# Hybrid encoder with a mixture of experts: gathers for two rounds at a time, 19 weight slots for 17, light and heavy rounds alternating

## The chip, the cores and the metric

The kernel runs on one core of one Trainium2 chip. The metric is the device time of one execution in microseconds. Loads of weights are issued by SyncE (SP) into one queue, and 16 DMA engines move them; TensorE (PE) multiplies, VectorE (DVE), ScalarE (ACT) and GpSimd (POOL) do the rest.

## The reference

Two layers are computed on 256 tokens of width 1024, in float32. Each layer first mixes tokens (a projection, banded attention, a state-space scan, retention, an output projection); then come 32 experts, of which each token uses the best two of its best group:

```python
for i in range(DEPTH):
    ...
    x = x + g1 * mixed
    h = _rmsnorm(x, norm2_g[i]) * (1.0 + sc2) + sh2
    x = x + g2 * _hier_moe(h, ...)
return _rmsnorm(x, final_g)

def _hier_moe(h, w_group, ..., w_down):
    group_idx = jnp.argmax(group_logits, axis=-1)
    ...
    top_val, top_idx = lax.top_k(in_group, TOP_K)       # 2 of the group's 8 experts
    ...
    for gi in range(N_GROUPS):
        hg = jnp.einsum('nd,edf->nef', t, w_gate[e])    # 1024 -> 256
        hu = jnp.einsum('nd,edf->nef', t, w_up[e])
        act = jax.nn.silu(hg) * hu * combine[:, e, None].astype(t.dtype)
        out = out + jnp.einsum('nef,efd->nd', act, w_down[e])   # 256 -> 1024
```

## The kernel before

Each layer has a mix phase and an expert phase. The expert phase of a layer reads all 32 experts: per expert two tiles of 1 MB with the gate and up weights (`wgu`, issued on L134) and one of 1 MB with the down weights (`moe_w_down`, L142), 96 loads in all. SP issues them in order in one queue. Each takes the next slot of a ring by turn (`wslot`, L120 to L128): 8 slots `ring2`, 7 slots `w`, 2 slots `ring3`, so 17. A slot is free again when the matmuls that read its last tile are done, and a load whose slot is not free holds up SP and every load behind it. In layer 0 eight loads for the next layer take the eight `ring2` slots first.

The expert phase begins with the routing (`route`): logits, the two experts of each token, and for each expert the place of each of its tokens. Experts are then worked off in 11 rounds, which fill 128 columns each: three fixed rounds with experts 0 to 5, two each with 64 token slots; then the other 26 experts, sorted by how many tokens they have (`order`, L1061 to L1100, 26x26 comparisons on DVE): three heavy rounds of two experts with 64 slots and five light rounds of four experts with 32 slots. So fixed and heavy rounds need 6 loads each and light ones 12. The order is fixed x 3, heavy x 3, light x 5. The sorted expert numbers (`numi`) are read into SP's registers by a TENSOR_LOAD (L1124); loads of experts 6 to 31 stand behind it in SP's queue and take their address from it.

Rounds take their tokens from blocks. A gather (L1142 to L1170) makes one: DVE writes a 0/1 matrix (`matrix`, L1109, in a `b4` buffer of 512 columns), PE multiplies the tokens with it (L1159; 32 matmuls, 8 row pieces of 128 x 4 terms), DVE and ACT write the result, scaled and shifted, into eight `b2` buffers of 128x512. Block 0 holds the three fixed rounds (256 columns ahead of round 0, 128 more behind its first product), block 1 rounds 3 to 6, block 2 rounds 7 to 10.

A round is then, on PE in the order written by `run` (L1266 to L1306): `slots` (two transposes, L1180, which give each slot's weight and the matrix for the way back), `gate_up` (L1195, 32 or 64 matmuls over 512 columns), `turned` (two transposes, L1207), `down` (L1220, 16 or 32 matmuls) and `scatter` (L1249 and L1250, 8 matmuls that add the result to the tokens). A fixed or heavy round's `down` comes behind the next round's `gate_up`, a light one's in its own round. Ahead of a gather the outstanding `down` is done, behind the gate and up product of the round the outstanding scatters.

After block 1 (round 6) stands the overflow branch (`between`, L1349 and on): a `tc.If` on the largest count (`cmi`), with the general code for experts with more than 64 tokens. On these inputs it isn't taken, but all engines evaluate it.

PE follows the program's order in the rounds; SP's loads are placed by the scheduler by when they become due, with loads of experts known ahead free to move forward, and those that need `numi` behind its TENSOR_LOAD.

Of the kernel before, what the change touches and what calls it, by code (L numbers as in the profile page):

```python
# [21 lines left out]
D = 1024  # L22
NE = 32
# [3 lines left out]
FIX, HEAVY, LIGHT = 6, 6, 32  # L27
DYN = NE - FIX
EPS = 1e-6
PRIO = 200  # L30
NW = 7
NW2 = 8
NW3 = 2

# [16 lines left out]
def body(tc, I, O):  # L51
# [3 lines left out]
    with tc.tile_pool(name="cp", bufs=1) as cp, tc.tile_pool(name="ring", bufs=NW) as ring, \  # L55
# [3 lines left out]
        def nm(s):  # L59
# [887 lines left out]
        def route(l, filler, scaled):  # L947
# [5 lines left out]
            def turned(h, t):  # L953
                xT[h, t] = b2([128, 512])
# [54 lines left out]
            m1, at1, f1 = first_max(ev, "a")  # L1009
            oh1, oh2 = sb([128, 10, 8], "oh1"), sb([128, 10, 8], "oh2")  # L1010
            V.tensor_tensor(oh1, at1, wide(f1), op=ALU.is_equal)
# [24 lines left out]

            def weights():
                V.tensor_tensor(oh2, at2, wide(f2), op=ALU.is_equal)
                m5 = m1.rearrange("p (t g) -> p t g", t=2)
# [13 lines left out]
                V.tensor_tensor(w2, w1, e, op=ALU.mult)  # L1053
                wa, both = sb([128, 10, 8], "wa"), sb([128, 10, 8], "both")
                for o, oh, w in ((wa, oh1, w1), (both, oh2, w2)):
# [5 lines left out]
            def order():  # L1061
# [8 lines left out]
                V.scalar_tensor_tensor(key, cnt[:, FIX:NE], 64.0, own, op0=ALU.mult, op1=ALU.subtract)  # L1070
                sq = [128, DYN, DYN]
                tmp, oh = sb(sq, "sqa"), sb(sq, "sqb")
# [4 lines left out]
                V.tensor_tensor(oh, C("iota")[:, 0:DYN].unsqueeze(2).to_broadcast(sq),  # L1077
                                rank[:, None, :].to_broadcast(sq), op=ALU.is_equal)

                def sorted_(dst, src):  # L1080
                    V.tensor_tensor(tmp, oh, src[:, None, :].to_broadcast(sq), op=ALU.mult)
                    V.tensor_reduce(dst, tmp, axis=AX.X, op=ALU.add)

# [29 lines left out]
        def experts(posm, comb, xhi, xlo, a2, sh2, gr2, l, ahead=True, D0=None, between=None, order=None, more=True,  # L1113
# [8 lines left out]
            if ahead:  # L1122
                numi, posd, comd = order
                _, num = nc.values_load_multi_w_load_instructions(  # L1124
                    numi[0:1, :], engines=(mybir.EngineType.SP,), min_val=FIX, max_val=NE - 1,
                    skip_runtime_bounds_check_because="sums of a permutation's 0/1 rows times FIX..NE-1")
                i = 0
                while i < NE:
                    n, w = (2, CAP) if i < FIX + HEAVY else (4, LIGHT)
                    r = len(rounds)  # L1130
# [4 lines left out]
                    i += n  # L1135
            else:
                for r in range(16):
                    j = slice(2 * r, 2 * r + 2)
                    rounds.append((r // 4, r % 4 * 128, CAP, posm[:, :, j], comb[:, :, j], [2 * r, 2 * r + 1]))
            last = {r[0]: i for i, r in enumerate(rounds)}  # L1140

            def gather(blk):  # L1142
                Dm[blk] = b4([128, 2, 512], F32R)
                for b, po, w, pos, _, _ in rounds:
                    if b == blk:
                        matrix(Dm[blk], po, pos, w)
                gathered(blk, slice(0, rounds[last[blk]][1] + 128), 1)

            def gathered(blk, ss, n):
                pc = {}  # L1150
                w = ss.stop - ss.start
                for c0 in range(0, 8, n):
# [17 lines left out]
            def slots(r):  # L1170
# [11 lines left out]
                V.tensor_reduce(cw, tp[:, 0:256], axis=AX.X, op=ALU.add)  # L1182
                sT = b1_([128, 256], F32R)
                V.tensor_scalar(sT, tp[:, 0:256], 0.0, None, op0=ALU.is_gt)
# [68 lines left out]
            if not ahead:  # L1253
                for r in range(16):
                    if r % 4 == 0:
                        gather(r // 4)
                    cw, sT = slots(r)
# [12 lines left out]
            def run(rs):  # L1270
                with tc.manual_schedule(engines={mybir.EngineType.PE}):
                    for r in rs:
                        blk, po, _, _, _, es = rounds[r]
                        if r == 0:
                            Dm[0] = D0
                            gathered(0, slice(0, 256), 4)
                        elif po == 0:
                            for q in list(aT):
                                downs(q)
                            gather(blk)  # L1280
                        cw, sTs[r] = slots(r)
                        act = gate_up(r, cw)
                        if r == 0:
                            gathered(0, slice(256, rounds[last[0]][1] + 128), 1)
                        if len(es) == 2:
                            scatters(0)
                            for q in list(aT):
                                downs(q)
                            aT[r] = turned(act)
                        else:  # L1290
                            for q in list(aT):
                                downs(q)
                            scatters(0)
                            aT[r] = turned(act)
                            if late and r == len(rounds) - 2:
                                late()
                            downs(r, r == len(rounds) - 1)
# [3 lines left out]

            half = last[1] + 1
            run(range(half))
# [3 lines left out]
        def moe(l, more):  # L1307
# [25 lines left out]
            with tc.manual_schedule(engines={mybir.EngineType.PE, mybir.EngineType.DVE}):  # L1333
                posm, comb, cmi, r, weights, order, less = route(l, filler, scaled)
                D0 = b4([128, 2, 512], F32R)
                matrix(D0, 0, posm[:, :, 0:4], CAP)
                for h in range(2):
                    hs = slice(h * 512, (h + 1) * 512)
                    for t in range(2):
                        V.scalar_tensor_tensor(xlo[:, t, hs], x[:, t, hs], r[:, t:t + 1], xhi[:, t, hs].bitcast(F32),  # L1340
                                               op0=ALU.mult, op1=ALU.subtract)
                matrix(D0, 4 * CAP, posm[:, :, 4:FIX], CAP)
            weights()
            ordered = order()

            def overflow():

                n = nc.values_load(cmi[0:1, 0:1], min_val=0, max_val=S)
                with tc.If(n > CAP):  # L1349
                    posr = sb([128, 2, 32], "posr")  # L1350
                    V.tensor_tensor(posr, posm, less.unsqueeze(1).to_broadcast([128, 2, 32]), op=ALU.add)
# [173 lines left out]
```

## Time and profile before

| | us |
|---|---|
| three runs | 867.43, 869.19, 874.86 (median 869.19) |
| the profiled execution | 867.36 |
| its span, first to last instruction | 865.5 |
| PE busy in the span | 723.1 (84%) |
| DVE busy | 486.2 (56%) |
| ACT busy | 240.4 (28%) |
| POOL busy | 110.2 (13%) |
| moved by DMA | 293.62 MB, mean 339 GB/s |

The profiled execution took 867.36 us, of which 865.5 us lie between the first and the last instruction, and its figures are those of the rows below. Layer 0's expert phase lies at about 193 to 436 us of the span, layer 1's at about 603 us to the end. A matmul is counted as busy from its start to its modelled end, so a high busy share of PE says that PE rarely waited, not that it ran at its peak. The granted clock of 1.00 is 2.4 GHz, and 0.50 would be 1.2 GHz; a figure between is a stretch that had both.

### The profile page before, as it was taken

What the parts mean: (1) busy time and instruction counts of PE and PEld (TensorE: products, weight loads), DVE (VectorE), ACT (ScalarE), POOL (GpSimd) and SP (SyncE); (2) the same over time, 40 slices, a digit from 0 to 9 for tenths busy, and PEclk for the clock granted to TensorE, in tenths of its full rate; (3) what the DMA queues carried; (4) which work ended last, traced back from release to release, by engine and by line L of the source; (5) the groups of instructions that cost most, each with busy time, mean ns of one, the idle gap of its engine ahead of it and who ended that gap; (6) DMA issues with size and microseconds to landing.
All of it is one profiled execution on the core that took longest, in us unless ns stands there. A gap on an engine that the chain in (4) does not pass through costs nothing. (4 is left out here: it accounts for less than half of the span.)

```text
span 865.5 us, 11404 instructions
## 1 busy us (share of the span) xinstructions
PE 723.1 (84%) x4110; PEld 389.5 (45%) x4110; DVE 486.2 (56%) x1075; ACT 240.4 (28%) x512; POOL 110.2 (13%) x163
## 2 busy tenths in 40 slices
PE   3698998898999985987678889879699998597864
PEld 0365775675444333322127558557644433232211
DVE  6689898457555344222058989944855535332114
ACT  1532334833112110200034323394321211020102
POOL 0453050002000000000035213100100000000000
PEclk9699999999999996989898989999799999699898
DMA  9977688969999889999999747669279988999992
GB/s 370 422 298 294 232 310 330 379 223 382 385 421 364 343 343 415 388 420 415 415 417 399 292 148 280 235 273 375 114 269 420 379 321 341 416 391 420 415 416 101
DMA packets 52037, 293.62 MB, mean 339 GB/s; under 512 B 4736, under 2 KB 4992, under 8 KB 26624
## 3 DMA queue, kind: packets, MB, share of 16 engines
q1 hardware_dynamic: 49536, 287.78, 83.8%
q10 hardware_dynamic: 2432, 4.98, 1.5%
q8 instruction: 36, 0.59, 0.3%
q14 instruction: 33, 0.27, 0.1%
HBM read 289.60 MB, written 1.05 MB: 336 GB/s over the span
## 5 line engine op out<-in xcount | busy, mean ns | idle before, releaser
L1195 PE MATMUL mm<-ring,b 128*32 128x512 f32 (+1 forms) x584 | 116.3, 603 | 14.3 <-DMA ring<-in_wgu_dram 14.3
L1195 PE MATMUL mm<-w,b 128*32 128x512 f32 (+1 forms) x440 | 98.7, 659 | 10.7 <-DMA w<-in_wgu_dram 10.7
L707 DVE TENSOR_TENSOR wh<-w,wh 128x512 fp32r<-128x512 f32 x120 | 89.2, 757 | 30.5 <-ACT wh L706 29.9
L1201 DVE SCALAR_TENSOR_TENSOR b<-mm,cw,b 128x256 f32<-128x256 f32 x22 | 10.6, 483 | 168.5 <-ACT b L1199 168.5
L706 ACT ACTIVATE wh<-w 128x512 fp32r<-128x512 f32 x120 | 74.4, 630 | 87.2 <-PE mm L731 48.3
L731 PE MATMUL mm<-wh,early 128*128 128x512 f32 x288 | 82.3, 432 | 6.5 <-ACT b L868 6.5
L1220 PE MATMUL sc<-ring,b 128*32 128x512 f32 (+1 forms) x312 | 67.8, 616 | 7.7 <-ACT b L1209 4.0
L731 PEld LDWEIGHTS mm<-wh,early 128*128 128x128 f32 x288 | 55.9, 204 | 31.8 <-ACT b L868 8.4
L1195 PEld LDWEIGHTS mm<-ring,b 128*32 128x32 f32 (+1 forms) x584 | 31.1, 121 | 77.5 <-issue 50.7
L204 PE MATMUL ac<-w,cc 128*32 128x512 f32 x320 | 46.6, 667 | 19.3 <-DVE cc L198 11.6
L1199 ACT ACTIVATE b<-mm 128x256 f32<-128x256 f32 x22 | 8.4, 384 | 188.9 <-PE mm L1195 188.9
L1229 DVE TENSOR_TENSOR y<-sc,gr 128x512 f32<-128x512 f32 x44 | 30.4, 691 | 49.9 <-PE sc L1220 48.3
L1195 PEld LDWEIGHTS mm<-w,b 128*32 128x32 f32 (+1 forms) x440 | 25.6, 130 | 67.0 <-issue 44.1
L1234 ACT ACTIVATE y<-y 128x512 fp32r<-128x512 f32 x40 | 25.2, 630 | 95.6 <-DVE y L1229 86.4
L726 PE MATMUL mm<-early,wh 128*128 128x256 f32 x384 | 50.5, 286 | 0.1
L1220 PE MATMUL sc<-w,b 128*32 128x512 f32 (+1 forms) x200 | 46.6, 669 | 4.7 <-DMA w<-in_moe_w_down_dram 3.1
L726 PEld LDWEIGHTS mm<-early,wh 128*128 128x128 f32 x384 | 46.9, 188 | 6.1 <-issue 4.5
L731 PE MATMUL mm<-wh,big 128*128 128x512 f32 x192 | 47.7, 399 | 1.4 <-DVE y L911 1.4
L1159 PE MATMUL tr<-b,big 128*128 128x512 f32 (+2 forms) x128 | 31.9, 392 | 19.5 <-DVE b L1109 19.1
L1175 POOL TENSOR_TENSOR b<-b,comd 128x128 f32<-128x128 f32 x32 | 12.8, 424 | 277.3 <-DVE b L1109 118.1
L731 PEld LDWEIGHTS mm<-wh,big 128*128 128x128 f32 x192 | 35.1, 189 | 9.2 <-DVE y L911 2.2
L1159 PEld LDWEIGHTS tr<-b,big 128*128 128x128 f32 x128 | 24.0, 223 | 27.4 <-issue 22.5
(349 smaller groups left out, 1095.1 us busy)
## 6 DMA issues: line engine op xcount, KB each, us to landing
ring<-in_wgu_dram SPq DMA_DIRECT2D x73, 1024.0 KB, 11.0
w<-in_wgu_dram SPq DMA_DIRECT2D x55, 1024.0 KB, 10.0
w<-in_w_ada_dram SPq DMA_DIRECT2D x40, 1024.0 KB, 10.4
ring<-in_moe_w_down_dram SPq DMA_DIRECT2D x39, 1024.0 KB, 13.6
w<-in_moe_w_down_dram SPq DMA_DIRECT2D x25, 1024.0 KB, 12.7
w<-in_win_dram SPq DMA_DIRECT2D x22, 1024.0 KB, 7.5
w<-in_w_out_dram SPq DMA_DIRECT2D x8, 1024.0 KB, 8.0
ring<-in_w_ada_dram SPq DMA_DIRECT2D x8, 1024.0 KB, 8.3
```

The costliest lines, as they stand in the source:

```text
L204: PE.matmul(acc[32 * t:32 * t + 32, :], c1[:, k:k + 1].to_broadcast([128, 32]), w[:, t * 512:(t + 1) * 512], start=(k == 0), stop=(k == 7) ...
L706: A.activation(wh[:, 0], w, AF.Copy)
L707: lo_eng[par_[0] % len(lo_eng)].tensor_tensor(wh[:, 1], w, wh[:, 0].bitcast(F32), op=ALU.subtract)
L726: PE.matmul(pt[t][:, f * 256:(f + 1) * 256], whs[i][:, w_, fs], a[x_][:, k], start=first and f + m == 0, stop=end and m == 2, skip_group_c ...
L731: PE.matmul(pt[t], a[x_][:, k, ts_], whs[i][:, w_], start=first and m == 0, stop=end and m == 2)
L1159: PE.matmul(pc[c], (xlo if i else xhi)[:, t, cs], Dm[blk][:, t, ss], start=(i + t == 0), stop=(i + t == 3))
L1175: G.tensor_tensor(Dc[:, t].rearrange("p (e s) -> p e s", s=w), Dm[blk][:, t, po:po + 128].bitcast(F32).rearrange("p (e s) -> p e s", s=w), ...
L1195: PE.matmul(gu[o:o + w, :], hg[blk, k][:, po + o:po + o + w], ws[k // 4][j][:, k % 4] if ahead else part_gu(l, es[j], k), start=(k == 0), ...
L1201: V.scalar_tensor_tensor(act, gu[:, 256:512], cw, si, op0=ALU.mult, op1=ALU.mult)
L1220: PE.matmul(yp[h][o:o + w, :], aT[:, f * 128 + o:f * 128 + o + w], wd[j][:, f, h] if ahead else part_wd(l, es[j], f, h), start=(f == 0), s ...
L1229: V.tensor_tensor(y, yp[h], gr2[:, h * 512:(h + 1) * 512], op=ALU.mult)
L1234: A.activation(yh, y, AF.Copy)
```

## The change

Six things change.

The ring gets two more `ring3` slots, 19 for 17. The memory comes from the blocks: the matrix `D` has 256 columns for 512 (two buffers), the gathered tokens `hg` 256 (eight buffers), and other small buffers are shared.

A block holds two rounds for four, so there are six gathers of 256 columns (the last of 128) for three and a half of 512.

The rounds stand in the order fixed x 3, light, heavy, light, heavy, light, heavy, light, light (`ORDER`). The overflow branch comes after round 7 (`HALF = 3`) for round 6.

The ranking is done in halves of 13 rows (338 elements) with twice the instructions, in `y2` buffers, which the rounds' outputs use later.

In `run` outstanding scatters are issued before the outstanding `down` and before a gather, and once more in a light round. The last round's gather is a block of its own, ahead of round 10.

The final norm's gain is broadcast (`late`) in front of the last round's `slots`, where it stood in the second last light round.

```diff
+HALF = 3
+ORDER = ["fixed"] * 3 + ["light", "heavy"] * 3 + ["light"] * 2
...
-NW3 = 2
+NW3 = 4
...
-                "moe": {"ring2": NW2, "ring3": NW3, "big": 2, "b4": 1, "b2": 8, "y2": 4, "b1": 8, "cw": 3},
+                "moe": {"ring2": NW2, "ring3": NW3, "big": 2, "D": 2, "hg": 8, "y2": 4, "b1": 4, "sT": 3, "cw": 3},
...
-                V.tensor_tensor(tmp, key[:, None, :].to_broadcast(sq), key.unsqueeze(2).to_broadcast(sq), op=ALU.is_ge)
-                V.tensor_reduce(rank, tmp, axis=AX.X, op=ALU.add)
...
+                for hv in halves:
+                    V.tensor_tensor(tmp, key[:, None, :].to_broadcast(sq), key[:, hv].unsqueeze(2).to_broadcast(sq),
+                                    op=ALU.is_ge)
+                    V.tensor_reduce(rank[:, hv], tmp, axis=AX.X, op=ALU.add)
...
-                    blk, po = (0, r) if i < FIX else (1 + (r - FIX // 2) // 4, (r - FIX // 2) % 4)
...
+                for r, kind in enumerate(ORDER):
+                    i, n, w = at_[kind], *((4, LIGHT) if kind == "light" else (2, CAP))
+                    at_[kind] += n
+                    blk, po = r // 2, r % 2
...
-                Dm[blk] = b4([128, 2, 512], F32R)
+                Dm[blk] = sb([128, 2, 256], "D", F32R)
...
-                            hg[blk, c] = b2([128, 512])
+                            hg[blk, c] = sb([128, 256], "hg")
...
                         elif po == 0:
+                            scatters(0)
                             for q in list(aT):
                                 downs(q)
                             gather(blk)
+                        if late and r == len(rounds) - 1:
+                            late()
                         cw, sTs[r] = slots(r)
                         act = gate_up(r, cw)
-                        if r == 0:
-                            gathered(0, slice(256, rounds[last[0]][1] + 128), 1)
-                        if len(es) == 2:
+                        scatters(0)
+                        for q in list(aT):
+                            downs(q)
+                        aT[r] = turned(act)
+                        if len(es) == 4:
                             scatters(0)
...
                             downs(r, r == len(rounds) - 1)
...
-            half = last[1] + 1
+            half = last[HALF] + 1
...
-                matrix(D0, 4 * CAP, posm[:, :, 4:FIX], CAP)
```

The first place is SP's queue at the start of layer 1's expert phase, where the loads of known experts end. Before, this stood there, with the TENSOR_LOAD of `numi` behind the 18th expert load:

```order
L134 DMA w_7722<-in_wgu_dram 128x2048
L142 DMA w_7762<-in_moe_w_down_dram 128x2x1024
L142 DMA ring_2040_7764<-in_moe_w_down_dram 128x2x1024
L142 DMA ring_2051_7793<-in_moe_w_down_dram 128x2x1024
L142 DMA ring_2052_7795<-in_moe_w_down_dram 128x2x1024
L1124 TENSOR_LOAD numi_7414
L134 ISA
L134 DMA ring_2081_7893<-in_wgu_dram 128x2048
```

In the changed kernel this stands there; lines have moved, so L137 is the load of gate and up weights, L145 that of down weights, and L1139 the TENSOR_LOAD:

```order
L137 DMA w_8148<-in_wgu_dram 128x2048
L137 DMA w_8150<-in_wgu_dram 128x2048
L137 DMA w_8152<-in_wgu_dram 128x2048
L137 DMA ring_2166_8154<-in_wgu_dram 128x2048
L1356 TENSOR_LOAD cmi_7728
L1356 ISA x2
L1139 TENSOR_LOAD numi_7783
L137 ISA
L137 DMA ring_2180_8208<-in_wgu_dram 128x2048
```

The TENSOR_LOAD of `numi` now has 16 expert loads ahead of it for 18: the two down loads of the third fixed round have moved behind the gate and up loads of the light round that follows. That of `cmi` (L1356) now stands directly ahead. In layer 0 it is 16 for 18 too.

The second place is DVE in layer 0's ranking, up to the cast that makes `numi`. Before:

```order
L1081 TENSOR_TENSOR sqa_2042<-sqb_2043,cst 128x676
L1096 TENSOR_TENSOR cnt_2038<-cnt_2038,less_2003 128x32
L1168 TENSOR_SCALAR b_440_2176<-ac_2158,a_337_1692,modT_97 128x256
L1082 TENSOR_REDUCE num_2048<-sqa_2042 128x26
L1098 TENSOR_REDUCE cm_2066<-cnt_2038 128x1
L1182 TENSOR_REDUCE cw_2186<-tr_2183 128x1
L1087 CAST numi_2051<-num_2048 128x26
L1081 TENSOR_TENSOR sqa_2042<-sqb_2043,posm_1983 128x676
L1099 CAST cmi_1985<-cm_2066 128x1
```

After, with the products L1096 and the sums L1097 for L1081 and L1082:

```order
L1097 TENSOR_REDUCE num_2050<-y_418_2040 128x13
L1111 TENSOR_TENSOR cnt_2036<-cnt_2036,less_2002 128x32
L1182 TENSOR_SCALAR hg_2188<-ac_2170,a_337_1692,modT_97 128x256
L1096 TENSOR_TENSOR y_418_2040<-y_420_2042,cst 128x338
L1113 TENSOR_REDUCE cm_2078<-cnt_2036 128x1
L1196 TENSOR_REDUCE cw_2198<-tr_2195 128x1
L1097 TENSOR_REDUCE num_2050<-y_418_2040 128x13
L1114 CAST cmi_1984<-cm_2078 128x1
L1198 TENSOR_SCALAR sT_2200<-tr_2195 128x256
L1102 CAST numi_2055<-num_2050 128x26
L1096 TENSOR_TENSOR y_418_2040<-y_419_2041,posm_1982 128x338
```

The cast now stands behind a second product and a second sum, the cast of `cmi` and round 0's `sT` (L1198, before L1184), which came behind it.

The third place is PE at the first gather that needs sorted experts. Before, it makes 512 columns for rounds 3 to 6, directly behind a `down` (L1220):

```order
L1220 MATMUL sc_2429<-w_2432,b_512_2426 64x512
L1220 MATMUL sc_2429<-ring_515_2430,b_512_2426 64x512
L1220 MATMUL sc_2429<-w_2432,b_512_2426 64x512
L1159 MATMUL tr_2463<-b_523_2454,big_1862 128x512 x2
L1159 MATMUL tr_2463<-b_523_2454,big_1863 128x512 x2
L1159 MATMUL tr_2470<-b_523_2454,big_1862 128x512 x2
```

After, the second such gather (L1173) makes 256 columns for rounds 4 and 5, behind the scatter of a light round (L1263 and L1264):

```order
L1263 MATMUL tr_2625<-y_568_2613,sT_2477 128x512
L1264 MATMUL tr_2625<-y_569_2615,sT_2477 128x512
L1263 MATMUL tr_2629<-y_568_2613,sT_2477 128x512
L1264 MATMUL tr_2629<-y_569_2615,sT_2477 128x512
L1173 MATMUL tr_2638<-D_2633,big_1862 128x256 x2
L1173 MATMUL tr_2638<-D_2633,big_1863 128x256 x2
L1173 MATMUL tr_2645<-D_2633,big_1862 128x256 x2
L1173 MATMUL tr_2645<-D_2633,big_1863 128x256 x2
```

The gather comes more often, with half the columns, and behind more of the outstanding work.

## Rows read from the trace of the kernel before

**Rows 1.** Windows: us, busy us by engine (instructions), clock, DMA share, GB/s

```profile
226.00:317.00 91.00, 88.52 (x427) 36.78 (x426) 39.25 (x74) 15.45 (x29) 3.95 (x10) 0.98 0.93 374
317.00:324.00 7.00, 4.65 (x22) 2.02 (x25) 5.19 (x9) 1.01 (x2) 0.00 (x0) 0.81 0.74 280
324.00:436.00 112.00, 83.46 (x462) 29.25 (x454) 31.06 (x56) 11.22 (x20) 3.23 (x8) 0.87 1.01 411
360.00:436.00 76.00, 59.30 (x330) 16.86 (x318) 18.90 (x33) 6.08 (x12) 0.76 (x2) 0.91 1.02 416
613.00:635.00 22.00, 15.31 (x76) 10.36 (x77) 20.23 (x59) 6.07 (x12) 3.16 (x5) 0.69 0.18 62
638.00:732.00 94.00, 90.09 (x436) 37.75 (x435) 41.61 (x78) 16.40 (x31) 3.95 (x10) 0.98 0.92 376
732.00:740.00 8.00, 6.97 (x39) 2.12 (x38) 3.74 (x7) 1.01 (x2) 0.00 (x0) 0.79 0.82 307
740.00:849.00 109.00, 79.42 (x458) 30.24 (x461) 29.91 (x55) 11.78 (x21) 3.23 (x8) 0.91 0.99 402
770.00:845.00 75.00, 57.03 (x342) 18.39 (x342) 18.67 (x33) 8.01 (x16) 1.51 (x4) 0.95 1.02 416
```

**Rows 2.** Windows of two short stretches, same columns

```profile
281.00:284.00 3.00, 3.00 (x16) 0.98 (x14) 0.00 (x0) 0.00 (x0) 0.00 (x0) 1.00 0.00 0
693.00:697.00 4.00, 4.00 (x20) 1.16 (x18) 0.00 (x0) 0.00 (x0) 0.00 (x0) 0.94 0.10 14
```

**Rows 3.** Waits of SP's queue, layer 0: us in total, times, longest us

```profile
SPq L134 <- PE mm L1195: 55.3, 9, 15.0
```

**Rows 4.** Waits of SP's queue, layer 1

```profile
SPq L134 <- PE mm L1195: 56.4, 10, 15.2
```

**Rows 5.** SP's timeline, layer 0: start us, us, instruction

```profile
219.93 0.37 SPq L142 DMA_DIRECT2D w<-in_moe_w_down_dram  x1
222.68 10.09 SPq L134 DMA_DIRECT2D w<-in_wgu_dram  x5
```

**Rows 6.** SP's timeline, layer 1

```profile
608.61 24.25 SPq L142 DMA_DIRECT2D ring<-in_moe_w_down_dram  x3
635.34 2.27 SPq L134 DMA_DIRECT2D ring<-in_wgu_dram  x3
```

**Rows 7.** Line 1124, load of expert numbers: ns min/median/max, first and last start

```profile
L1124 SPq TENSOR_LOAD <-numi x2: 1848/1954/2059, 220.4 to 632.9; - x2
```

**Rows 8.** SP's one load at 219.93 us, issue to landing

```profile
DMA to landing us min/median/max: 6.2/6.2/6.2
```

**Rows 9.** VectorE's timeline, ranking of layers 0 and 1

```profile
218.32 0.17 DVE L1087 CAST numi<-num 128x26 int32<-128x26 f32 x1
...
219.23 0.42 DVE L1184 TENSOR_SCALAR b<-tr 128x256 fp32r<-128x256 f32 x1
...
628.93 0.17 DVE L1087 CAST numi<-num 128x26 int32<-128x26 f32 x1
```

**Rows 10.** TensorE's timeline, one heavy round

```profile
290.23 0.44 PE L1207 MATMUL mm<-cst,b 128*128 128x128 f32 x2
...
290.81 7.09 PE L1195 MATMUL mm<-ring,b 128*64 128x512 f32 x32
297.83 0.50 PE L1249 MATMUL ac<-y,b 128*128 128x512 f32 x1
...
299.57 0.39 PE L1250 MATMUL tr<-y,b 128*128 128x512 f32 x1
299.89 3.65 PE L1220 MATMUL sc<-ring,b 128*64 128x512 f32 x16
```

**Rows 11.** TensorE's timeline, gathers of 512, of 256 and of 128 columns

```profile
262.06 2.00 PE L1159 MATMUL ac<-b,big 128*128 128x512 f32 x8
...
627.35 1.05 PE L1159 MATMUL ac<-b,big 128*128 128x256 f32 x4
...
636.77 1.06 PE L1159 MATMUL ac<-b,big 128*128 128x128 f32 x8
```

More of the change, by code (lines that the diff above doesn't have):

```diff
@@ L953, in turned @@
             def turned(h, t):
-                xT[h, t] = b2([128, 512])
+                xT[h, t] = y2([128, 512])
                 p = ps("tr")
@@ L1009, in route @@
             m1, at1, f1 = first_max(ev, "a")
-            oh1, oh2 = sb([128, 10, 8], "oh1"), sb([128, 10, 8], "oh2")
+            oh1 = sb([128, 10, 8], "oh1")
             V.tensor_tensor(oh1, at1, wide(f1), op=ALU.is_equal)
@@ L1037, in weights @@
             def weights():
+                oh2 = sb([128, 10, 8], "aa")
                 V.tensor_tensor(oh2, at2, wide(f2), op=ALU.is_equal)
@@ L1053, in weights @@
                 V.tensor_tensor(w2, w1, e, op=ALU.mult)
-                wa, both = sb([128, 10, 8], "wa"), sb([128, 10, 8], "both")
+                wa, both = sb([128, 10, 8], "ev2"), sb([128, 10, 8], "at3")
                 for o, oh, w in ((wa, oh1, w1), (both, oh2, w2)):
@@ L1126, in experts @@
                     skip_runtime_bounds_check_because="sums of a permutation's 0/1 rows times FIX..NE-1")
[L1127 to L1130, printed above, removed]
-                    blk, po = (0, r) if i < FIX else (1 + (r - FIX // 2) // 4, (r - FIX // 2) % 4)
+                at_ = {"fixed": 0, "heavy": FIX, "light": FIX + HEAVY}
+                for r, kind in enumerate(ORDER):
+                    i, n, w = at_[kind], *((4, LIGHT) if kind == "light" else (2, CAP))
+                    at_[kind] += n
+                    blk, po = r // 2, r % 2
                     j = slice(i - FIX, i - FIX + n) if i >= FIX else slice(i, i + n)
@@ L1138, in experts @@
                     j = slice(2 * r, 2 * r + 2)
-                    rounds.append((r // 4, r % 4 * 128, CAP, posm[:, :, j], comb[:, :, j], [2 * r, 2 * r + 1]))
+                    rounds.append((r // 2, r % 2 * 128, CAP, posm[:, :, j], comb[:, :, j], [2 * r, 2 * r + 1]))
             last = {r[0]: i for i, r in enumerate(rounds)}
             def gather(blk):
-                Dm[blk] = b4([128, 2, 512], F32R)
+                Dm[blk] = sb([128, 2, 256], "D", F32R)
                 for b, po, w, pos, _, _ in rounds:
@@ L1182, in slots @@
                 V.tensor_reduce(cw, tp[:, 0:256], axis=AX.X, op=ALU.add)
[L1183 removed]
+                sT = sb([128, 256], "sT", F32R)
                 V.tensor_scalar(sT, tp[:, 0:256], 0.0, None, op0=ALU.is_gt)
@@ L1254, in experts @@
                 for r in range(16):
-                    if r % 4 == 0:
-                        gather(r // 4)
+                    if r % 2 == 0:
+                        gather(r // 2)
                     cw, sT = slots(r)
@@ L1280, in run @@
                             gather(blk)
+                        if late and r == len(rounds) - 1:
+                            late()
                         cw, sTs[r] = slots(r)
                         act = gate_up(r, cw)
-                        if r == 0:
-                            gathered(0, slice(256, rounds[last[0]][1] + 128), 1)
-                        if len(es) == 2:
-                            scatters(0)
[L1287 to L1296, printed above, removed]
+                        scatters(0)
[3 more added lines that the diff above has]
+                        if len(es) == 4:
+                            scatters(0)
                             downs(r, r == len(rounds) - 1)
@@ L1334, in moe @@
                 posm, comb, cmi, r, weights, order, less = route(l, filler, scaled)
-                D0 = b4([128, 2, 512], F32R)
+                D0 = sb([128, 2, 256], "D", F32R)
                 matrix(D0, 0, posm[:, :, 0:4], CAP)
```

21 lines of the change are left out of this document (13 added, 8 removed).

## Prediction

> **What bounds the kernel now.** I read the windows first [rows 1]. Late in each expert phase DMA runs at 416 GB/s for 75 us (360 to 436, 770 to 845), and PE is busy for only 59.3 of 76 and 57.0 of 75 us: there the weights set the pace. At 416 GB/s a tile of 1.0486 MB takes 2.52 us. Earlier in the same phases it is not so. From 226 to 317 DMA moved 374 GB/s and PE was busy for 88.5 of 91 us; from 638 to 732 it was 376 GB/s and 90.1 of 94. PE is full there, the weights come late because of it, and the two limits take turns. The reader sees the link in short windows: 281 to 284 at 0 GB/s, 693 to 697 at 14, with PE busy throughout and at a clock of 1.00 and 0.94 [rows 2]. SP's waits tell what stopped it: 55.3 and 56.4 us for matmuls of L1195, the gate and up products, which free slots [rows 3, 4]. Most of those waits cost nothing, since SP issues ahead of the transfers; what counts is the bytes missing from the windows.
>
> So three heavy rounds behind three fixed ones want about as much PE as DMA (a round needs 6 tiles, 15.1 us), and five light ones want 30 us of DMA each and much less PE. With 17 slots the surplus of the one kind can't be lent to the other.
>
> **The missing bytes.** Against 416 GB/s, 226:317 loses 91 x (1 - 374/416) = 9.2 us and 638:732 loses 94 x (1 - 376/416) = 9.0 us. The windows behind the overflow branch lose 2.3 (317:324) and 2.1 us (732:740), then 1.35 (324:436) and 3.7 us (740:849) [rows 1]. The first two of these four are SP starting again behind the branch, which stays, so nothing is taken from them. Of the last two, 5.0 us together, part is slots and part the same restart; I take 2.0, with 0 and 5.0 as bounds.
>
> **What the change does about them.** A pair of a light and a heavy round needs 18 tiles, 45.4 us. On PE [rows 10] it costs two gate and up products (7.09 each), two downs (3.65), two scatters (8 matmuls from 297.83 to 299.96, 2.13) and twice the transposes of `turned` and `slots` (290.23 to 290.81, 0.6): 27 us. To this comes one gather. The new one of 256 columns has 32 matmuls: with 512 columns eight take 2.00 us and a quarter of a gather thus 1.9, 7.6 in all; with 128 columns eight take 1.06, about 3.8 in all; with 256, at a mean clock of 0.69 in that stretch, four take 1.05 [rows 1, 11]. I take the middle of the bounds, 5.7. PE needs 33 us in 45, so in pairs the weights bound every stretch, not two rounds in a row alone. The 19 slots hold more than a pair's 18 tiles. I therefore take the losses of 226:317 and 638:732 as gone: 9.2 + 9.0 + 2.0 = 20.2 us saved, at most 23.2, and at least half of the 18.2, 9.1, if the three fixed rounds that still stand in a row keep theirs.
>
> Six gathers come for four products (two of 512, one of 256, one of 128 columns): about 5 x 5.7 + 3.8 = 32 us of PE for 7.6 x 2 + 5.7 + 3.8 = 25 per layer. The 7.6 us more lie in PE's idle time, 17 us in 360:436 and 18 us in 770:845 [rows 1]; without that cover both layers would pay 15 us. The earlier scatters wait for outputs that DVE and ACT make, under the same cover. DVE itself is busy for 42 of 94 us at most. The last round's own gather stands ahead of its 8 gate and up tiles, 20 us of transfer, in which 3.8 us of PE vanish. The tail behind the last tile keeps its steps and is priced at nothing.
>
> **What it gives back.** SP stops at the TENSOR_LOAD of `numi`, and only 16 expert loads stand ahead of it for 18. So all three further slots stay empty until `numi` is there, and the ring's growth brings nothing in that gap; DMA does two tiles fewer before it. In 613:635 it moved only 62 GB/s [rows 1].
>
> Layer 0: before, the 18th load was issued at 219.93 [rows 5] and landed 6.2 us later [rows 8], at 226.1; the first that needs `numi` was issued at 222.68, 2.3 us after the TENSOR_LOAD at 220.4 [rows 5, 7]. `numi` itself was cast by 218.5 [rows 9], so a slot held SP up, not the ranking. Now no slot does, and the ranking counts. Five operations become ten, each split at no more than the smallest operation's 0.17 us, 0.85; round 0's `sT` (0.42) and the cast of `cmi` (0.17) now stand ahead of the cast [rows 9]. That is 1.4 us, `numi` at 219.9, the first load at about 222.3, its landing at 228.5. But it is the 17th: the 18th follows at 231.0. Lost: 4.9 us.
>
> Layer 1: before, the 18th load was issued at 632.49 (the last 0.37 us of the row that ends at 632.86) and the next at 635.34 [rows 6]. `numi` was cast by 629.1 [rows 9], and will be by 630.5. Ahead of its TENSOR_LOAD now stands that of `cmi`. One takes 1.85 to 2.06 us [rows 7]; `cmi` is cast 0.6 us before `numi`, so about 1.4 us of it count if the two don't overlap. First load at 630.5 + 1.4 + 2.4 = 634.3, landing at 640.5, the 18th at 643.0 against 632.49 + 6.2 = 638.7. Lost: 4.3 us, or 2.9 if the loads overlap.
>
> **The sum.** 20.2 - 4.9 - 4.3 = 11.0 us saved. The profiled execution took 867.36 us, 1.8 under the median of the runs, so 856.4 for it and about 858 for the median. In layer 0 the saving passes through the next mix phase whole, as its first loads already follow the last expert tile in the queue. Bounds: 23.2 saved and only 5.0 lost (the two tiles) gives 18 and 851 for the median, 849 beside the profiled execution; 9.1 saved and 9.2 lost gives no change.
>
> A rule of the Trainium skill speaks against the whole gain: "DMA: Bandwidth & Descriptors", in its opening table and the section "Where 436 GB/s comes from", puts what one core can draw from HBM at about 358 GB/s. By it 374 GB/s would already be the limit, nothing would be saved and 9 us lost. The windows at 416 GB/s over 75 us, which are loads from HBM, exclude it here, so it gets no chance.
>
> **Rivals.** *PE stays the bound, no change.* PE's 97% in 226:317 is its own fill, and the three fixed rounds with the light round's first product behind them keep it full for some 60 us, whatever the slots. Then half of the 18.2 us stays: 11.0 - 9.1 = 2, a median of 867. For it speaks that PE, not DMA, is full in those windows; against it that over 226 to 436 PE is busy for 177 of 210 us in all (184 with the gathers' 7.6), and 79 tiles need 199. Chance 0.32, with all between 860 and 868 in it.
>
> *The clock takes it, slower.* In pairs PE would wait for tiles all along, and its clock could fall in these waits. With a gather at its upper bound a pair is 34.6 us of PE at 2.4 GHz, and PE becomes the bound once the mean granted clock is below 34.6/45.4 = 0.76. At 0.69, the clock of the thin stretch 613:635, a pair takes 50 us, 4.7 more than its tiles; with 80 tiles per layer there are 8.9 pairs in both, 42 us, a median of 900; with gathers of 5.7 us it is 18 us and 876. Against it: the stretches of before in which DMA is the bound were granted 0.91 and 0.95 [rows 1]. Chance 0.09, and 0.02 for other losses. The Trainium skill describes such a case in "TensorE: Matmul & The Clock Gate", section on HAM oscillation: waits for DMA between short bursts of matmuls throttle the clock again and again. The 0.91 and 0.95 of this trace show little of it.
>
> *The start costs nothing more.* `numi` comes in time, only two tiles are lost: 15 us saved, a median of 854. Chance 0.1; it counts with the forecast below 860.
>
> **How the numbers follow.** The forecast (850 to 860) has 0.47, with the rival on its side 0.57. About 1%, 8.7 us, is what a measurement of this kernel can tell from no change; so faster by more (below 860.5) has 0.57, within it 0.32, slower 0.11. The range is 849 to 868: the lower end is the sum's best bound, the upper the rival in which half the loss stays; outside lie the slower cases and what is above or below by other causes, 0.16.
>
> **What would show it.** Right: 400 GB/s or more, and no empty stretch of 3 us, from the first load behind `numi` to the branch, in both layers; PE busy for about 75% there; the first load behind `numi` at about 222.3 in layer 0, and in layer 1 about 4 us behind the cast of `numi`. Wrong: empty windows behind the third fixed round, PE at 95% or more in the pairs, or a clock below 0.76 in them.

## The result, and the profile after

The changed kernel took 861.88 us (median of 4 runs, 858.3 to 863.92) against 868.64 us for the kernel before, a ratio of 0.989 with a 95% interval of 0.9843 to 0.9938. Run again beside other kernels it took 860.6 us, a ratio of 0.9893 (0.9861 to 0.9925). So the change is worth about 1.1%, 9 us by the ratios and 7 to 8 by the medians, where 858 us had been forecast, in the range of 849 to 868. The sign, the place of the gain ahead of the branch and the range held. The size of the saving and both losses at the start came out otherwise than the sum had them. One run of the kernel before without its branch (869.18 us) was in a slower state than its others and is left out of its median below.

The profiled execution took 862.21 us, with a span of 860.4. These are windows of it, in the columns of [rows 1]:

```profile
222.00:228.00 6.00, 5.72 (x31) 2.24 (x31) 5.90 (x20) 2.32 (x3) 0.82 (x2) 1.00 0.00 0
233.00:362.00 129.00, 116.98 (x680) 48.19 (x679) 55.59 (x104) 21.76 (x42) 4.55 (x12) 0.99 1.02 417
364.00:371.00 7.00, 0.97 (x3) 0.49 (x3) 1.59 (x3) 0.00 (x0) 0.00 (x0) 0.69 0.70 250
616.00:633.00 17.00, 11.81 (x61) 8.01 (x63) 16.59 (x57) 4.50 (x9) 1.96 (x4) 0.70 0.01 1
638.00:766.00 128.00, 115.88 (x676) 47.52 (x674) 54.62 (x102) 21.76 (x42) 4.55 (x12) 0.99 1.02 417
771.00:777.00 6.00, 0.72 (x3) 0.70 (x4) 1.55 (x5) 0.00 (x0) 0.92 (x2) 0.50 0.77 300
843.00:860.40 17.40, 7.25 (x34) 2.33 (x34) 7.43 (x15) 4.22 (x10) 0.73 (x1) 0.84 0.16 61
```

Where the kernel before moved 374 and 376 GB/s with PE full [rows 1], the changed one moves 417 without a break from the first loads behind `numi` to the branch, 129 and 128 us long. The empty stretches of [rows 2] are gone. Two kinds of gap are left: the wait for `numi` (222:228 at 0 GB/s, 616:633 at 1), and the restart behind the overflow branch (250 and 300 GB/s in 364:371 and 771:777). The tail is as long as it was. SP waits less than half as long for the gate and up products as in [rows 3, 4]; waits of SP's queue in layer 0, then in layer 1, where L1357 is the branch, at which SP waits for its loads to land:

```profile
SPq L137 <- PE mm L1209: 26.6, 11, 6.5
SPq L1357 <- SPq L1357: 18.4, 8, 2.6
```

```profile
SPq L137 <- PE mm L1209: 22.5, 9, 5.9
...
SPq L1357 <- SPq L1357: 18.2, 2, 17.8
```

A pair of rounds on PE, from its timeline: the gather of 256 columns, the heavy round's product, and the next pair's gather; ahead of them two of a scatter's matmuls, which now wait for their outputs:

```profile
280.30 0.49 PE L1263 MATMUL tr<-y,sT 128*128 128x512 f32 x1 [0.49 <-ACT y L1248]
281.43 0.51 PE L1264 MATMUL tr<-y,sT 128*128 128x512 f32 x1 [0.64 <-DVE y L1250]
...
290.38 1.33 PE L1173 MATMUL tr<-D,big 128*128 128x256 f32 x8 [0.31 <-DVE x L1265]
...
293.47 1.12 PE L1173 MATMUL ac<-D,big 128*128 128x256 f32 x8
294.43 0.38 PE L1194 MATMUL tr<-cst,b 128*128 128x128 f32 x2
294.74 7.09 PE L1209 MATMUL mm<-ring,hg 128*64 128x512 f32 x32
```

```profile
326.10 1.34 PE L1173 MATMUL tr<-D,big 128*128 128x256 f32 x8 [0.32 <-DVE x L1265]
```

A gather takes 4.1 us (290.38 to the transposes at 294.43), and a pair 35.7 us (290.38 to 326.10). All waits of PE from 233 to 362:

```profile
PE mm L1221 <- DVE b L1215: 4.6, 3, 2.5
PE tr L1264 <- DVE y L1250: 3.7, 6, 0.6
PE tr L1263 <- ACT y L1248: 3.1, 6, 0.6
PE sc L1234 <- SPq L1357: 1.7, 2, 1.5
PE tr L1194 <- DVE x L1265: 0.7, 1, 0.7
PE tr L1173 <- DVE x L1265: 0.6, 2, 0.3
```

The row of the branch's line is the wait for the last down tiles ahead of it, from about 356 us on. Before that PE waits for no tile: it has its own path to work off, as the stream has.

### The profile page after: what moved, and what is told of

The parts are those of the page before. It is cut to its first block, busy times and chain, and to the rows that moved or that the text cites. A ratio compares the mean times of both kernels' runs of the same rounds, so it can differ in the third digit from the quotient of the medians.

```text
span 860.4 us, 11665 instructions
## 1 busy us (share of the span) xinstructions
PE 716.6 (83%) x4238; PEld 396.1 (46%) x4238; DVE 492.3 (57%) x1117; ACT 245.5 (29%) x528; POOL 110.8 (13%) x163
## 5 line engine op out<-in xcount | busy, mean ns | idle before, releaser
L1209 PE MATMUL mm<-ring,hg 128*32 128x512 f32 (+1 forms) x656 | 114.9, 606 | 3.6 <-DMA ring<-in_wgu_dram 3.6
L1209 PE MATMUL mm<-w,hg 128*64 128x512 f32 (+1 forms) x368 | 76.6, 604 | 0.0
L1209 PEld LDWEIGHTS mm<-ring,hg 128*32 128x32 f32 (+1 forms) x656 | 32.3, 120 | 62.0 <-issue 54.6
L1234 PE MATMUL sc<-w,b 128*32 128x512 f32 (+1 forms) x200 | 51.5, 616 | 3.6 <-DMA w<-in_moe_w_down_dram 3.5
L1173 PE MATMUL tr<-D,big 128*128 128x256 f32 (+1 forms) x192 | 34.9, 326 | 19.5 <-DVE D L1124 15.0
L1189 POOL TENSOR_TENSOR b<-D,comd 128x128 f32<-128x128 f32 x32 | 12.5, 410 | 298.5 <-PE tr L1194 116.0
L1173 PEld LDWEIGHTS tr<-D,big 128*128 128x128 f32 x192 | 29.7, 221 | 26.9 <-issue 17.0
L1209 PEld LDWEIGHTS mm<-w,hg 128*64 128x64 f32 (+1 forms) x368 | 22.6, 125 | 39.9 <-issue 38.6
```

Of the source, the lines that this page charges most:

```text
L1173: PE.matmul(pc[c], (xlo if i else xhi)[:, t, cs], Dm[blk][:, t, ss], start=(i + t == 0), stop=(i + t == 3))
L1189: G.tensor_tensor(Dc[:, t].rearrange("p (e s) -> p e s", s=w), Dm[blk][:, t, po:po + 128].bitcast(F32).rearrange("p (e s) -> p e s", s=w), ...
L1209: PE.matmul(gu[o:o + w, :], hg[blk, k][:, po + o:po + o + w], ws[k // 4][j][:, k % 4] if ahead else part_gu(l, es[j], k), start=(k == 0), ...
L1234: PE.matmul(yp[h][o:o + w, :], aT[:, f * 128 + o:f * 128 + o + w], wd[j][:, f, h] if ahead else part_wd(l, es[j], f, h), start=(f == 0), s ...
```

## Experiments

Each kernel ran beside the kernel before on one chip. "Holes" are the time by which tiles landed later than one every 2.51 us, added up tile by tile over those that came more than 0.3 us late. A stretch's loss is the whole time that it took beyond one tile every 2.51 us, from the landing of its first tile to that of its last.

| kernel | median us | ratio to before | 95% interval |
|---|---|---|---|
| changed, again | 860.6 | 0.9893 | 0.9861 to 0.9925 |
| changed, 17 slots | 860.2 | 0.9913 | 0.9866 to 0.996 |
| changed, order of before | 862.19 | 0.992 | 0.9886 to 0.9953 |
| changed, 17 slots and order of before | 871.38 | 1.0016 | 0.9981 to 1.0052 |
| before, new order only | 861.07 | 0.9883 | 0.9794 to 0.9971 |
| changed, no branch | 851.14 | 0.9804 | 0.9761 to 0.9847 |
| before, no branch | 858.75 | 0.9886 | 0.9839 to 0.9932 |
| changed, branch behind round 1 | 872.66 | 1.0067 | 1.0037 to 1.0097 |
| changed, two tiles first | 860.1 | 0.9899 | 0.985 to 0.9947 |
| changed, less PE work | 862.03 | 0.9914 | 0.9877 to 0.9952 |
| two tiles first, less PE work | 854.02 | 0.9803 | 0.9736 to 0.987 |
| two tiles first, two light rounds early | 859.04 | 0.9854 | 0.9772 to 0.9935 |

**Which part brings the gain: slots or order?** Three kernels take back one part or both.

```diff
-NW3 = 4
+NW3 = 2
```

> The changed kernel with two ring3 slots for four, so 17 slots in all; order, gathers and ranking stay. Theory A (the alternating order takes the holes away, the slots add little): the losses against 2.51 us a tile between the 18th tile and the branch stay under 3 us per layer, and the time is within 3 us of the changed kernel, 859 to 865. Theory B (the two slots do it): the holes come back with 6 to 9 us per layer, and the time is 872 to 880.

```diff
-ORDER = ["fixed"] * 3 + ["light", "heavy"] * 3 + ["light"] * 2
+ORDER = ["fixed"] * 3 + ["heavy"] * 3 + ["light"] * 5
```

> The changed kernel with the rounds in the order of before (fixed x 3, heavy x 3, light x 5); 19 slots, gathers of two rounds and the ranking in halves stay, and the branch stays behind round 7, which is now the second light round. Theory A (the order does it): losses of 6 to 9 us per layer ahead of the branch come back, 872 to 880 us. Theory B (the two slots do it): losses under 3 us per layer, 859 to 865 us.

Both edits together:

> The changed kernel with 17 slots and the order of before: what is left of the change are the gathers of two rounds, the ranking in halves and the scatters ahead of the downs. If those are hidden or cost nothing it takes as long as the kernel before, 866 to 872 us; if they cost PE time where PE is full, 875 to 885 us, with losses of 10 us or more per layer ahead of the branch.

And the kernel before with the order alone, in its blocks of four rounds:

```diff
-                    n, w = (2, CAP) if i < FIX + HEAVY else (4, LIGHT)
...
+                for r, kind in enumerate(ORDER):
+                    i, n, w = at_[kind], *((4, LIGHT) if kind == "light" else (2, CAP))
+                    at_[kind] += n
```

> The kernel before with nothing changed but the order of its rounds (fixed x 3, light, heavy, light, heavy, light, heavy, light, light); 17 slots, blocks of four rounds, the ranking whole, the branch behind round 6. Theory A (order alone is enough, as 19 slots alone were): the holes of 8.5 us per layer ahead of the branch shrink to under 5, and the time is 857 to 863 us. Theory B (the smaller blocks are needed too, since a gather of four rounds stops PE for 7.6 us at once): 866 to 871.

Windows from the first loads behind `numi` to near the branch, both layers, columns as above; 17 slots, then order of before, then both, then the order alone in the kernel before:

```profile
230.00:355.00 125.00, 113.19 (x671) 48.33 (x668) 52.24 (x95) 20.75 (x40) 4.54 (x12) 0.98 1.02 416
640.00:765.00 125.00, 112.72 (x663) 48.02 (x659) 52.18 (x93) 21.37 (x41) 4.55 (x12) 0.99 1.02 417
```

```profile
236.00:350.00 114.00, 108.33 (x622) 47.39 (x618) 51.69 (x95) 20.82 (x41) 4.55 (x12) 0.99 1.01 412
643.00:755.00 112.00, 106.34 (x616) 46.91 (x616) 51.96 (x96) 20.34 (x40) 4.55 (x12) 1.00 1.02 417
```

```profile
236.00:350.00 114.00, 107.85 (x614) 47.13 (x614) 50.77 (x93) 20.30 (x40) 4.55 (x12) 0.99 0.99 399
650.00:765.00 115.00, 108.52 (x620) 47.34 (x615) 52.39 (x96) 20.94 (x41) 4.55 (x12) 1.00 1.00 404
```

```profile
229.00:325.00 96.00, 91.31 (x492) 37.01 (x493) 41.23 (x76) 15.66 (x29) 3.96 (x10) 0.96 1.00 407
636.00:730.00 94.00, 89.17 (x493) 36.43 (x492) 42.55 (x78) 15.74 (x30) 3.97 (x10) 1.00 1.01 410
```

With 17 slots the stream still moves 416 and 417 GB/s; with the old order but 19 slots 412 and 417; only with both taken back does it fall to 399 and 404, and the gain is gone (ratio 1.0016). So neither theory was right alone: the order is enough without the slots, and the slots are nearly enough without the order. The account that fits all four is that what was in short supply is how far SP may run ahead of PE while heavy rounds follow each other, and that either part covers it. In the kernel before, the new order alone does the same, 407 and 410 GB/s and a ratio of 0.9883, with gathers of four rounds: the smaller blocks, the ranking in halves and the earlier scatters weren't needed for the gain. The slots alone were not run in the kernel before, since the smaller blocks give them their memory. The other parts don't cost anything that shows either: with both other parts taken back, what is left takes as long as the kernel before (1.0016, at most 1.0052).

**What the branch costs.** The call of `between()` is left out, in both kernels:

```diff
             run(range(half))
-            between()
             run(range(half, len(rounds)))
```

> The changed kernel without the overflow branch (the code for experts with more than 64 tokens is left out, which these inputs don't enter); the rounds are still cut in two at the same place. In the changed kernel's trace the tiles behind the branch lose 4.9 us in layer 0 and 6.1 in layer 1. Theory A (SP's wait for all loads and the restart of the stream cost that, in a stage that the weights bound): these losses go, and the time falls by 9 to 11 us, to 851 to 854. Theory B (PE's 8 us stop at the branch, not the stream, sets the time there, or the next limit takes over): it falls by under 4 us, to 858 or more.

> The kernel before without its overflow branch (left out as well). Its tiles behind the branch lose about 4.4 us in layer 0 and 2.9 in layer 1. If the branch costs the kernel before less than the changed one, it falls by 4 to 7 us, to 862 to 865. If it costs both the same, it falls by 9 to 11, to 858 to 860.

The changed kernel without it streams through, both layers:

```profile
230.00:425.00 195.00, 170.88 (x987) 72.43 (x984) 75.95 (x142) 30.90 (x60) 6.82 (x18) 0.97 1.02 417
636.00:830.00 194.00, 171.37 (x990) 77.67 (x986) 75.49 (x139) 31.87 (x62) 6.83 (x18) 0.96 1.02 417
```

It is 9.5 to 10.7 us faster by the medians and 7.7 by the ratios (0.9893 - 0.9804). The kernel before gets 9.6 us faster by the medians (868.39 on that chip) and 9.9 by the ratio. So theory A holds, and the branch costs both kernels about the same, 8 to 11 us, which is near the 11.0 us that the tiles behind it lose in the changed kernel's trace (4.9 and 6.1).

Can the stop be put where SP waits anyway? The branch was moved behind round 1, with the fixed rounds' 18 loads ahead of it:

```diff
...
-            half = last[HALF] + 1
+            half = 2
             run(range(half))
+            es = rounds[2][5]
+            early_gu[2] = [[load_gu(l, e, h) for e in es] for h in range(2)]
+            early_wd[2] = [load_wd(l, e) for e in es]
             between()
```

> The changed kernel with the overflow branch behind round 1 for round 7 and all 18 tiles of the fixed rounds issued ahead of it, so that SP's wait for its loads falls into the gap in which it waits for `numi` anyway. Theory A: the 4.9 and 6.1 us behind the branch go, and the two tiles in the gap give 5 us per layer: 843 to 848 us. Theory B: PE stops at the branch for 8 us where it has the least time to spare, slots come free late, and 6 to 10 us of the gain are given back in holes before the first heavy round: 852 to 858.

```profile
230.00:310.00 80.00, 62.81 (x348) 28.75 (x348) 33.50 (x68) 12.63 (x24) 3.20 (x8) 0.91 0.86 348
262.00:271.00 9.00, 9.00 (x50) 4.32 (x49) 1.84 (x4) 1.70 (x3) 0.76 (x2) 0.98 0.22 66
642.00:712.00 70.00, 56.62 (x311) 26.13 (x312) 32.26 (x64) 11.12 (x21) 2.44 (x6) 0.93 0.83 334
```

It is slower than both kernels, beyond what theory B allowed. No tile is late where the branch had been, but the stream falls to 348 and 334 GB/s in the first rounds, and to 66 GB/s from 262 to 271 with PE busy for all 9.0 us: PE had stopped at the branch, stood behind the stream, and freed no slot in time (SP's longest wait for a gate and up product is 25.0 us there, 6.5 in the changed kernel). The stop costs more there, where PE is short, than behind round 7, where the weights are: from the first tile behind `numi` to the last of the layer the loss is 15.6 us in each layer, against 6.7 and 7.4 in the changed kernel.

**What the two tiles behind `numi` cost.** They are issued with the third fixed round's gate and up tiles:

```diff
...
                         act = gate_up(r, cw)
+                        if r == 2:
+                            early_wd[2] = [load_wd(l, e) for e in es]
```

> The changed kernel with the two down tiles of the third fixed round issued straight behind its gate and up tiles, so that 18 expert loads stand ahead of the TENSOR_LOAD of `numi`, as before the change. Theory A (the stream is the bound from there on, so two tiles more in the gap are worth two tiles in each layer): 8 to 10 us less than the changed kernel, 852 to 854. Theory B (behind the gap PE sets the pace, or the two tiles would only wait): within 3 us of it, 859 to 865.

```profile
232.00:350.00 118.00, 108.65 (x636) 45.36 (x636) 49.80 (x95) 20.14 (x39) 4.57 (x12) 0.99 0.98 399
277.00:281.00 4.00, 2.88 (x13) 1.36 (x10) 3.18 (x5) 1.27 (x3) 0.00 (x0) 1.00 0.62 180
642.00:755.00 113.00, 103.95 (x618) 45.31 (x616) 46.37 (x85) 19.13 (x37) 4.56 (x12) 0.97 0.99 404
```

The ratio is 0.9899, that of the changed kernel. The two tiles do come earlier, but the stream then falls to 399 and 404 GB/s, with a hole of its own from 277 to 281 at 180. Theory B holds: what is won ahead of `numi` is lost again ahead of the branch. PE waits for tiles 0.2 us at most in the two long windows, so it is on its own path there. Whether PE's pace takes the gain or the slots do, two kernels with less PE work should tell, the changed one and this one; half of the scatters' matmuls are left out (the low part of the outputs, so the result is less exact):

```diff
-                            PE.matmul(p, to, yh, start=True, stop=False)
-                            PE.matmul(p, to, yl, start=False, stop=True)
+                            PE.matmul(p, to, yh, start=True, stop=True)
```

> The changed kernel with half of the scatters' matmuls left out (the low part of each output, so the result is less exact); about 0.9 us of PE less per round, 10 us per layer. If the stream alone sets the time from the first load behind `numi` to the end, the time stays, 858 to 864 us; if PE sets part of it, it falls by 4 us or more.

> The kernel with the two down tiles ahead of the TENSOR_LOAD (a_wdfirst), with the same half of the scatters' matmuls left out. That kernel's stream began two tiles ahead and lost them again in holes of 5 to 6 us per layer ahead of the branch. If those holes are PE's pace, 4 to 5 us of PE less ahead of them shrink them, and it is 4 to 8 us under a_wdfirst, 852 to 856 us; if they are only the number of slots and where each comes free, it stays at 858 to 862.

The changed kernel first, then the one with the two tiles:

```profile
230.00:355.00 125.00, 107.53 (x634) 44.07 (x630) 53.08 (x96) 22.00 (x42) 4.57 (x12) 0.97 1.01 415
638.00:760.00 122.00, 104.75 (x616) 41.11 (x616) 50.44 (x91) 20.91 (x40) 4.56 (x12) 0.99 1.02 417
```

```profile
228.00:350.00 122.00, 107.27 (x621) 43.96 (x620) 52.71 (x99) 21.08 (x41) 4.57 (x12) 0.96 0.99 406
636.00:755.00 119.00, 104.38 (x614) 44.21 (x614) 50.62 (x91) 20.90 (x40) 4.56 (x12) 0.96 1.00 409
```

Less PE work does nothing for the changed kernel (0.9914, 415 and 417 GB/s): there the stream alone sets the time from `numi` to the branch. With the two tiles ahead the median falls by 6 us (854.02 against 860.1), but the intervals of the two ratios overlap, and in the two traces the clock of layer 0's routing differs as well, without the cut and with it:

```profile
197.00:215.00 18.00, 17.37 (x105) 9.22 (x104) 7.08 (x36) 2.96 (x6) 1.57 (x1) 0.66 0.90 334
```

```profile
197.00:215.00 18.00, 16.16 (x134) 9.46 (x132) 12.23 (x48) 5.36 (x12) 3.52 (x4) 1.00 1.02 417
```

In the second the TENSOR_LOAD of `numi` starts at 220.1 us for 225.0, which is not PE's work behind it. Behind it, from the first tile that needs `numi` to the layer's last, the stream takes 2.4 us less in each layer (202.6 and 201.5 for 205.0 and 203.9). The loss ahead of the branch falls from 6.5 and 5.0 us to 4.7 and 3.8; in the changed kernel it is 1.4. So PE's pace, its waits for outputs included, is the next limit, some 4 to 5 us per layer behind the first; that it takes all of these is not shown, since less PE work gave back 1 to 2 of them ahead of the branch.

The same kernel with a second light round ahead of the heavy ones, which asks less of PE per tile:

```diff
-ORDER = ["fixed"] * 3 + ["light", "heavy"] * 3 + ["light"] * 2
+ORDER = ["fixed"] * 3 + ["light"] + ["light", "heavy"] * 3 + ["light"]
```

> The kernel with the two down tiles ahead of the TENSOR_LOAD, with two light rounds behind the fixed ones (fixed x 3, light, light, heavy, light, heavy, light, heavy, light), so that PE has less to do per tile where it was full. Theory A (PE's pace behind three fixed rounds takes the two tiles back): the holes of 5 to 6 us shrink and it is 850 to 856 us, faster than both kernels. Theory B (the three fixed rounds alone fill PE, whatever follows): 858 to 862.

```profile
232.00:350.00 118.00, 107.60 (x638) 44.87 (x638) 51.13 (x97) 20.20 (x39) 4.56 (x12) 0.99 0.98 400
642.00:755.00 113.00, 103.10 (x624) 44.29 (x622) 48.34 (x89) 19.81 (x38) 4.57 (x12) 0.98 0.99 403
```

400 and 403 GB/s are those without that edit. The median of 859.04 is the lowest of the kernels that compute everything, but its interval covers the changed kernel's ratio; it is no version that can be called better. Theory B fits: an easier round behind the first light one changes nothing, so the holes are made by the rounds ahead of it.

**Is layer 0's late start the change's doing?** In the changed kernel's trace the first load behind `numi` left at 228.15 us, not at 222.3. The kernel was run again as it is:

> The changed kernel once more, as it is. In its first profile the first load behind `numi` left at 227.95 us in layer 0, where 222.3 was predicted; the routing there ran at half the clock for a while and the mix phase before it was 1.9 us longer. Theory A (chance of the granted clock, not the change): in this profile that load leaves at 221 to 226 us or elsewhere again, and differs from 227.95 by more than 1 us; the median lies at 858 to 864. Theory B (the change itself makes the routing slower, by its ranking in halves): it leaves at 227.5 to 228.5 again.

The TENSOR_LOAD of `numi` (first and last start: layers 0 and 1), the clock in 197:215 and 16 small matmuls of the routing, as far as each view has them, in the changed kernel, in its repeat, and in the one with 17 slots, whose instructions are the same up to there but for the slots of its loads:

```profile
L1139 SPq TENSOR_LOAD <-numi x2: 1847/1945/2043, 225.8 to 630.8; - x2
```

```profile
197.00:215.00 18.00, 17.09 (x109) 9.14 (x109) 7.38 (x37) 4.32 (x11) 2.28 (x2) 0.72 0.95 367
```

```profile
L1139 SPq TENSOR_LOAD <-numi x2: 1847/1945/2043, 224.4 to 631.5; - x2
```

```profile
201.57 3.64 PE L965 MATMUL sc<-prb,y 128*128 128x40 f32 x16
```

```profile
L1139 SPq TENSOR_LOAD <-numi x2: 1847/1949/2051, 220.3 to 629.8; - x2
```

```profile
197.00:215.00 18.00, 16.16 (x133) 9.56 (x133) 12.19 (x50) 5.36 (x12) 3.51 (x4) 1.00 0.94 355
```

```profile
200.63 1.98 PE L965 MATMUL sc<-prb,y 128*128 128x40 f32 x16
```

The repeat gave 224.4, 1.4 us earlier; 17 slots gave 220.3. Over the eleven traces of kernels with the changed ranking the layer 0 clock in 197:215 is either 1.00 or 0.66 to 0.72, and 16 small matmuls of the routing take 1.98 or 3.64 us. At 1.00 the TENSOR_LOAD starts at 217.5 to 220.4 (four traces, and a fifth in which it stands behind the moved branch), at the lower level at 224.4 to 226.3 (six). The ranking in halves is in all of them, so it alone isn't the cause, and the kernel before without its branch, which ranks as before, reads alike in its trace (the run of 869.18 us), with the TENSOR_LOAD at 226.3:

```profile
197.00:215.00 18.00, 17.43 (x105) 9.25 (x104) 7.13 (x35) 2.96 (x6) 1.57 (x1) 0.67 0.66 244
```

By its measure, more than 1 us, theory A holds. But the repeat had the lower clock too (0.72), so that one and the same program runs at either level is not shown. What tips the clock in this stretch stays open: from 180 to 197 the repeat and the kernel with 17 slots both have a clock of 1.00 and PE busy for 14.4 us.

## Why the prediction was right, and where it wasn't

**What bounds the kernel** was right. The weights' stream with holes made by PE and slots was the bound, the holes went, and the stream now runs at 417 GB/s, where the late windows of before had 416. That less PE work changes nothing shows it directly. Of the signs that were named, 400 GB/s or more and no empty stretch came true; PE's 75%, the first load of layer 0 at 222.3 and the 4 us behind the cast of `numi` in layer 1 (2.6 measured) did not.

**The saving** was put at 20.2 us. Counted by tiles, the 78 tiles from the 18th to the last took 210.0 and 210.2 us before and 202.5 and 203.2 after: 14.4 us. So 5.8 us are missing, most of them ahead of the branch. There the term was right in kind and too large: the loss was 8.3 us in each layer before and is 1.4 after, so 13.8 us came of the 18.2. The two windows of GB/s had read it 1.6 too high, and 1.4 per layer stays, most of it in one tile that lands 3.7 and 3.8 us behind the one ahead of it (at 256.8 and 659.2), in a stretch that still moves 409 GB/s (253 to 257); no experiment takes it away. Behind the branch I left 4.4 us as the price of the restart and took 2.0 of the other 5.0 for slots. The loss there was 5.9 and 6.1 us before and is 5.3 and 6.1 after, so 0.6 came. Without a branch it is 0.5 us or less in either kernel: these losses were the branch's, and little of them could go.

**What it gives back** came to the forecast's size by two errors. In layer 0 the 18th tile landed 9.5 us later than before (4.9 forecast), 5 to 6 of it the clock in the routing, in which no part of the change is shown; in the traces with the clock at 1.00 the TENSOR_LOAD starts at 217.5 to 220.4, around the forecast 219.9. In layer 1, counted from layer 0's last tile, it landed 0.1 us earlier (4.3 late forecast). There the TENSOR_LOAD of `cmi` took 0.29 us, not 1.85 to 2.06:

```profile
L1356 SPq TENSOR_LOAD <-cmi x2: 289/292/296, 341.5 to 630.2; - x2
```

I had taken one price for two loads of unlike size, one number and 26. In both layers the first load behind `numi` landed 4.9 and 4.8 us after its issue, where I had taken the 6.2 of [rows 8], which are those of a down tile. And in layer 1 the counts came 1.5 us sooner behind layer 0's last tile than before, for which the record has no cause. That the two losses add up to 9.3 us, 9.2 forecast, is luck. The ranking, from the counts to `numi`, got longer by 0.5 us in layer 0 (10.33 to 10.87) and 1.0 in layer 1 (6.69 to 7.66), for 1.4 forecast.

**That two tiles behind `numi` cost 5 us per layer** was wrong in what it is worth, though the tiles did move. With them ahead the time is the same, since the stream then loses 4 to 5 us more in each layer ahead of the branch. The pair is not the cause: 33 us were forecast and 35.7 measured, and both are under the 45 us of its tiles. (The gather was cheaper than thought, 4.1 for 5.7, but a scatter behind its own down now waits for ACT and DVE, 0.5 and 0.6 us each.) What the working left out is how far PE is behind when the pairs begin. The three fixed rounds, which the first rival named, leave it a backlog that it works off almost up to the branch without a wait for tiles, as its waits above show, so it was busy for 117 of 129 us where about 75% was forecast.

**The sum** in the profiled executions: 14.4 saved and 9.3 given back, with a tail as long as before, makes 5.1 us of span, 865.5 to 860.4. Forecast were 11.0. By the medians it is 7 to 8. The profiled execution is one with the lower clock in layer 0, which would explain a part of that; the clocks of the other runs in this stretch are not on record.

**The rivals.** PE as the bound, with half the loss left, didn't come: 1.4 us of 8.3 are left in each layer. But PE is nearer than was said. The clock rival didn't come either: 0.99 in both streams. A start that costs no more than its two tiles came out for layer 1 alone.

**The rule on HBM** that was weighed, about 358 GB/s for one core in the Trainium skill ("DMA: Bandwidth & Descriptors", section "Where 436 GB/s comes from"), doesn't hold here, where one core runs: the windows above show 415 to 417 GB/s of reads from HBM. The 425 GB/s that the same section names for a 16 MB transfer is nearer.

## What to carry to other kernels

Where two engines take turns as the bound, first look for an order of the same work that lets them overlap: here a new order alone did as much, within the intervals, as the whole change with its two more buffers, smaller blocks and rewritten ranking. Parts that mend the same shortage don't add up, so try each alone and both undone. And before pricing a stall, ask what would be the bound without it: two tiles that came 5 us late per layer were free, because the stream lost them again behind PE, while the branch behind them cost its full 8 to 11 us.

## What the runs showed of the hardware

The routing of layer 0 ran at a granted clock of 1.00 in five of eleven traces and of 0.66 to 0.72 in the other six, in the same part of the program, and the layer's last tile landed later for it (438.1 and 436.6 us in the changed kernel's two traces, 433.5 with 17 slots). A restart of an emptied stream of 1 MB loads behind a branch cost 5 to 6 us per layer: SP's wait for all loads to land, then 5.3 and 5.5 us from the first issue to the first landing in the changed kernel's trace, then two tiles that came about 1 us late each.
